# A hybrid encoder on one core: the S5 mixer in chunks of four tokens instead of eight, two groups to a matmul

## The chip, the cores and the metric

The kernel runs on one core of one Trainium2 chip. The metric is the device time of one execution in microseconds (us). The core has five engines that run their own instruction queues in order: TensorE (PE in the profile; PEld is its loading of weights), VectorE (DVE), ScalarE (ACT), GpSimd (POOL) and SyncE (SP, which here only issues DMAs).

## The reference

A trunk of two layers works on 272 tokens (16 meta tokens and 256 inputs) of 2048 features in float32. Each layer has a token mixer, half of it attention and half of it a bidirectional S5 scan, and then a channel mixer, which is dense in layer 0 and two-of-eight experts in layer 1. The S5 half is what the change touches:

```python
def s5_direction(u_c, lam_re, lam_im, log_step, b_re, b_im, c_re, c_im, reverse):
    lam = lax.complex(lam_re, lam_im)                       # per group (64) and state (64)
    dt = jnp.exp(log_step)[:, None]
    lam_bar = jnp.exp(lam * dt)
    b_bar = ((lam_bar - 1.0) / lam)[..., None] * b          # states x 16 channels
    bu = jnp.einsum('gpc,blgc->blgp', b_bar, u_c)
    a = jnp.broadcast_to(lam_bar, bu.shape)
    _, h = lax.associative_scan(combine, (a, bu), axis=1, reverse=reverse)
    return jnp.real(jnp.einsum('gcp,blgp->blgc', c, h))     # 16 channels of each group
```

It runs forwards and backwards, the two are added with `d_skip * u`, and a gelu and a gate follow before the output projection.

## The kernel before

The program is five stages: layer 0's mixers (`mixer`), layer 0's output projection and dense mixer (`mixer_end`, `dense`), layer 1's mixers, its output projection with the router, and the experts (`moe`). Large products run as three float32r products of split weights and split inputs; weights stream from DRAM through `Stream` and are split by ACT (`wh`) and DVE (`wl`). In layer 0's mixers the weights are used as float32 as they come (`raw`).

The order of all instructions is fixed when the program is built. `Sched` runs one main generator and side generators, keeps a model of when each engine would get to the work, and lets a side task emit its next piece once its operands should be there. `LEAD` holds how far DVE may run ahead of TensorE for each side task. On the chip each engine then takes its instructions in that order, so an instruction that is not ready holds up all that stands behind it on its engine.

S5 works in chunks of `TC` = 8 tokens, `NC` = 34 chunks, for 64 groups of 16 channels, with 64 complex states in each direction (128 rows: forward states on partitions 0 to 63, backward on 64 to 127):

- `prep` makes powers 0 to 8 of the discretized eigenvalues, on DVE.
- `v_load` and `v_make` make V, a chunk's 8 x 16 inputs to the states, two groups at a time: two DMAs of 256 KB (`pscr` and `ssm_bT`) and four DVE products of 128 x 512 and 128 x 256.
- `ssm_x` multiplies V (128 x 128, real and imaginary) by the group's inputs U (128 x 34): what each chunk adds to the states, X.
- `ssm_scan` steps through the chunks on DVE: four products of 128 x 128 for each of the 32 steps. Each step needs the one before it.
- `w_all` makes W (states to outputs), and from it with small matmuls (`toep`, 64 x 160) M, a chunk's inputs to its own outputs. Both go through DRAM (`wscr`, `escr`, `mscr`).
- `ssm_y` makes each group's outputs with three matmuls, chunks on partitions: states before the chunk H (128 x 34) by W (128 x 128), twice, and U by M. `turn` transposes them.

For layer 1 V, W and M are made during layer 0's dense mixer (`ahead`) and read back (`ssm_v1`, `ssm_w`). In both layers x stands between the input products, the scan mostly within attention, and y within the first half of the output projection (`w_out`, half 0), ahead of the gate.

Of the kernel before, what the change touches and what calls it, by code (L numbers as in the profile page):

```python
# [9 lines left out]
F32 = mybir.dt.float32  # L10
# [14 lines left out]
NC = 34  # L25
TC = 8
VG = 2
SLACK = 6000.0
NRAW = 40
VQ = 3  # L30
XHEAD = 0
# [5 lines left out]
        "prep1": 400.0, "v1": 800.0, "w1": 700.0, "scan1": 100.0, "gate": 2125.0}  # L37
# [4 lines left out]
# the router's constants  # L42
MLOW, MTOK, MTRI, MIO = 0, 64, 72, 200
NMC = 328
# expert 0's first rows of features
# [19 lines left out]
class Arena:  # L65
    """Columns of one float32 tile, handed out and taken back in emission order."""
# [23 lines left out]
    def room(self, *ws):  # L90
        """Whether pieces of these widths can all be had."""
# [46 lines left out]
class Stream:  # L138
    """The weights in the order of use: loaded ahead, and split into two float32r parts unless they are
    taken as they are."""  # L140
# [63 lines left out]
    def tend(self):  # L204
        """What can be done ahead without a long wait."""
# [34 lines left out]
class Model:  # L240
    """When each engine gets to the work emitted so far, by what the work's operands wait for."""
# [9 lines left out]
    def where(self, ap):  # L251
        """The region of ap, in units of a few columns of a partition quarter."""
# [13 lines left out]
        else:  # L266
# [3 lines left out]
            if sb:  # L270
                row = n // tn.shape[0]
                p0, f0 = divmod(off, row)
                np_ = pat[0][1] if len(pat) else 1
# [22 lines left out]
    def ready(self, *aps):  # L296
        """When what was emitted will have been written into aps."""
# [7 lines left out]
    def clear(self, ap):  # L305
        """When what was emitted will be done with ap."""
# [68 lines left out]
class Eng:  # L375
    """An engine whose work is timed as it is emitted."""
# [68 lines left out]
class Sched:  # L445
    """Emission order: main work, with side work where its operands should be there.

    A generator yields None, a time of the tensor engine to wait for, a condition, or the name of
    a backlog of the vector engine to wait for."""
# [19 lines left out]
    def add(self, gen, urgent=None):  # L469
        """A side task; with urgent, one that fills idle time until urgent()."""  # L470
# [56 lines left out]
class Kern:  # L527
    def __init__(self, ctx, tc, A, out, dbg=None):
# [8 lines left out]
        self.pscr = [dp.tile([8, NG, 256], F32, name=f"pscr{l}") for l in range(2)]  # L537
        self.uscr = [dp.tile([8, 128, L], F32, name=f"uscr{l}") for l in range(2)]
        self.escr = [dp.tile([NG, 16, 240], F32, name=f"escr{l}") for l in range(2)]
        self.vscr = dp.tile([16, 128, 1024], F32, name="vscr")  # L540
        self.wscr = [dp.tile([16, 128, 1024], F32, name=f"wscr{l}") for l in range(2)]
        self.mscr = [dp.tile([128, NG, 128], F32, name=f"mscr{l}") for l in range(2)]
# [8 lines left out]
        self.Wp = self.pp.tile([128, 2, 10, NG], F32, name="Wp")  # L551
# [19 lines left out]
    def banks(self, **n):  # L571
        """Splits the banks of PSUM into rings."""
# [7 lines left out]
    def grab(self):  # L580
        """A bank of the shared ring that nobody holds."""
# [112 lines left out]
    def later(self, f, *aps):  # L694
        """Work whose operands are still being made."""
# [15 lines left out]
    def norm(self, ps, n, dst, flag):  # L711
        """dst = 1 / sqrt(ps + eps) once the sums in ps are there."""
# [1604 lines left out]
```

## Time and profile before

| what | before |
|---|---|
| median of 3 runs | 2624.03 us (2618.33 to 2628.5) |
| span of the profiled execution, first to last instruction | 2615.0 us |
| TensorE busy | 2540.2 us, 97% |
| DVE busy | 1950.8 us, 75% |
| ACT busy | 1349.5 us, 52% |
| mean granted TensorE clock | 0.986 |

No other time of the profiled execution is given; its span is 9.0 us under the median of the runs. All helpers record through one line (L403), so rows are told apart by operation, tile and shape. A float32 matmul has two records in the trace, a transpose one. "128*34 128x128" is a matmul with 128 rows, 34 columns of weights, and 128 columns that move. `fa` is the arena in which most tiles of S5 lie, `bank` a bank of PSUM.

### The profile page before, as it was taken

The page shows a single profiled execution, that of the slowest core. Times are in us where ns is not written, and L with a number is a line of the kernel's source. Part 1 is how long each engine was busy: PE and PEld are TensorE (multiplying, and loading weights), DVE is VectorE, ACT ScalarE, POOL GpSimd, SP SyncE. Part 2 cuts the span into 40 slices and gives each one's busy share as a digit, 9 for nine tenths or more (in the row PEclk, how much of TensorE's full clock was granted, in tenths as well). Part 3 has the DMA queues.
Part 4 walks back from the last instruction along what each step waited for, and adds up shares of the span by engine and source line. Part 5 has one row for each costly group of instructions (what it writes and reads, how often), then busy time and mean ns, then how long its engine had stood idle before and what let it go on. Part 6 is the DMA issues. An engine that isn't in the chain of part 4 may idle for free. (4 is left out here: it accounts for less than half of the span.)

```text
span 2615.0 us, 42822 instructions
## 1 busy us (share of the span) xinstructions
PE 2540.2 (97%) x16266; PEld 2276.0 (87%) x16266; DVE 1950.8 (75%) x3108; ACT 1349.5 (52%) x1850; POOL 12.7 (0%) x17
## 2 busy tenths in 40 slices
PE   8989999999999999999999999999999999999997
PEld 6766588999999999999999977898888888888886
DVE  7567883778777766666665476266999999999997
ACT  2112543543334333333344555355777777777775
POOL 0000000000000000000000000000000000000000
PEclk9998999999999999999999999999999999999998
DMA  6875275445888866566557724574999999999995
GB/s 210 201 213 182 75 244 195 159 161 179 276 272 276 268 196 213 192 200 213 191 171 216 213 105 149 174 292 165 381 342 385 358 341 386 354 336 374 356 342 194
DMA packets 266375, 637.36 MB, mean 244 GB/s; under 512 B 43489, under 2 KB 103265, under 8 KB 265009
## 3 DMA queue, kind: packets, MB, share of 16 engines
q1 hardware_dynamic: 263890, 622.42, 70.1%
q0 software_dynamic: 1552, 9.91, 1.1%
q8 instruction: 129, 2.11, 0.4%
q10 hardware_dynamic: 720, 2.23, 0.2%
q14 instruction: 84, 0.69, 0.1%
HBM read 599.85 MB, written 42.99 MB: 246 GB/s over the span
## 5 line engine op out<-in xcount | busy, mean ns | idle before, releaser
L403 DVE TENSOR_TENSOR wl<-raw,wh 128x1024 fp32r<-128x1024 f32 (+1 forms) x559 | 666.2, 1202 | 191.7 <-ACT wh L403 183.1
L403 ACT ACTIVATE wh<-raw 128x1024 fp32r<-128x1024 f32 (+1 forms) x559 | 579.4, 1040 | 307.0 <-PE bank L403 217.9
L403 PE MATMUL bank<-XH,wh 128*128 128x272 f32 (+1 forms) x2160 | 637.7, 295 | 0.5 <-ACT tmpr L403 0.5
L403 PE MATMUL bank<-XH,wl 128*128 128x272 f32 (+1 forms) x2160 | 623.4, 289 | 2.7 <-DVE wl L403 2.6
L403 PE MATMUL bank<-XL,wh 128*128 128x272 f32 (+1 forms) x2160 | 621.0, 287 | 1.6 <-DVE XL L403 1.3
L403 PEld LDWEIGHTS bank<-XH,wh 128*128 128x128 f32 x2160 | 407.4, 189 | 16.4 <-issue 14.5
L403 PEld LDWEIGHTS bank<-XH,wl 128*128 128x128 f32 x2160 | 407.2, 189 | 4.3 <-DVE wl L403 4.3
L403 PEld LDWEIGHTS bank<-XL,wh 128*128 128x128 f32 x2160 | 408.0, 189 | 2.5 <-DVE XL L403 2.2
L403 DVE TENSOR_TENSOR fa<-fa 128x256 f32<-128x256 f32 (+11 forms) x703 | 289.3, 425 | 108.9 <-DMA fa<-ssm_bT 60.2
L403 PE MATMUL bank<-fa 128*34 128x128 f32 (+10 forms) x2148 | 343.5, 302 | 25.3 <-DVE fa L403 17.9
L403 PEld LDWEIGHTS bank<-fa 128*34 128x34 f32 (+6 forms) x2148 | 267.9, 158 | 89.4 <-issue 33.6
L403 PE MATMUL bank<-ra,wh 128*128 128x272 f32 (+1 forms) x1792 | 342.9, 291 | 2.3 <-ACT wh L403 2.3
L403 ACT ACTIVATE fa<-bank 64x320 f32<-64x320 f32 (+8 forms) x281 | 138.4, 498 | 348.4 <-PE bank L403 315.2
L403 PEld LDWEIGHTS bank<-ra,wh 128*128 128x128 f32 x1792 | 281.8, 189 | 8.4 <-issue 4.6
L403 PE MATMUL bank<-ra,wl 128*128 128x272 f32 (+1 forms) x896 | 257.3, 287 | 0.8 <-DVE wl L403 0.8
L403 PE MATMUL bank<-wh,XH 128*128 128x512 f32 (+1 forms) x584 | 221.9, 380 | 0.7 <-ACT fa L403 0.4
L403 PE MATMUL bank<-wh,XL 128*128 128x512 f32 (+1 forms) x584 | 219.8, 376 | 0.0
L403 PE MATMUL bank<-wl,XH 128*128 128x512 f32 (+1 forms) x584 | 218.5, 374 | 0.0
L403 PE MATMUL bank<-wh,ra 128*128 128x512 f32 x552 | 185.0, 392 | 0.0
L403 PE MATMUL bank<-fa,raw 128*128 128x272 f32 x608 | 172.3, 425 | 8.5 <-DMA raw<-w_mix 7.4
L403 PEld LDWEIGHTS bank<-ra,wl 128*128 128x128 f32 x896 | 169.3, 189 | 1.0 <-DVE wl L403 1.0
L403 DVE TENSOR_TENSOR wl<-h,wh 128x1024 fp32r<-128x1024 f32 (+1 forms) x137 | 157.0, 1156 | 10.0 <-ACT wh L403 7.4
(118 smaller groups left out, 3053.2 us busy)
## 6 DMA issues: line engine op xcount, KB each, us to landing
raw<-w_dense SPq DMA_DIRECT2D x264, 512.0 KB
raw<-w_mix SPq DMA_DIRECT2D x150, 512.0 KB
raw<-w_moe_g SPq DMA_DIRECT2D x106, 512.0 KB
h<-w_moe_g SPq DMA_DIRECT2D x80, 512.0 KB
raw<-w_moe_d SPq DMA_DIRECT2D x73, 512.0 KB
h<-w_moe_d SPq DMA_DIRECT2D x59, 512.0 KB
raw<-w_moe_t SPq DMA_DIRECT2D x51, 384.0 KB
h<-w_moe_t SPq DMA_DIRECT2D x44, 384.0 KB
```

Of the source, the lines that this page charges most:

```text
L403: return f(*a, **k)
```

## The change

The chunk has four tokens (`TC` = 4, `NC` = 68). A group then has 4 x 16 = 64 input rows, and groups g and g + 32 share the 128 partitions: the rows of one at 0 to 63, of the other at 64 to 127. For x the inputs of both stand side by side with zeros in the other half (128 x 136), so one pair of matmuls serves two groups. The y matmuls stay three for each group, with 68 columns of weights (H, U) and 64 that move (W, M). The scan has 66 steps. `prep` needs powers 0 to 4. H is no longer one tile: `ssm_h` makes it for four groups at a time, with one copy of 64 x 536 on ACT and one on DVE, in a ring of two. U is loaded twice (`load_u`), for x and again for y, and the tiles of channels are taken in the order `TORD`. Two 128 x 1088 fills on POOL (`room_xu`) stand ahead of the first DMAs there. `LEAD` of the scan in layer 1 rises from 100 to 1200.

The program's instructions that change in number, both layers, before and after: x matmuls 256 and 128; y matmuls 384 and 384; `toep` matmuls 256 and 256; transposes of y 128 and 64; scan products on DVE 256 and 528; products of V 256 and 128; products of W 288 and 288 (of 320 or 640 columns, then 192 or 384); copies of X on ACT 64 and 128; copies into H 6 and 32 on either engine; DMAs on SP 2181 and 2037.

```diff
-NC = 34
-TC = 8
+NC = 68
+TC = 4
+NQ = NG // 2
+TORD = (0, 4, 1, 5, 2, 6, 3, 7)
+GW = (2, 4)
-        "prep1": 400.0, "v1": 800.0, "w1": 700.0, "scan1": 100.0, "gate": 2125.0}
+        "prep1": 400.0, "v1": 800.0, "w1": 700.0, "scan1": 1200.0, "gate": 2125.0}
...
+    def room_xu(self, F):
+        X = F.get([NC - 1, 2, NG], top=True)
+        U = Ring(Top(F), 2, [8, 2, NC])
+        for u in U.h:
+            self.nc.gpsimd.memset(u.ap, 0.0)
+        return X, U
+    def load_u(self, l, qb):
+        u = self.st["U"].next()
+        for hf in range(2):
+            self.nc.sync.dma_start(u[64 * hf:64 * hf + 64, :, hf],
+                                   rows(self.uscr[l], (4 * hf + qb) * 128 * L,
+                                        [[L, 16], [NC, TC], [16 * L, 8], [1, NC]]))
+        return u
...
-        for b in range(NG // VG):
+        for b in range(NQ // VG):
             pb, bt = got.pop(0)
             yield from self.v_make(l, v.ap, pb, bt)
...
+                    ps = bank[:, :4 * NC].rearrange("p (r h s) -> p r h s", r=2, h=2)
                     for r in range(2):
-                        nc.tensor.matmul(ps[:, g + i, r], v[:, i, r], U[:, b * 4 + g + i], start=True, stop=True)
+                        nc.tensor.matmul(ps[:, r].rearrange("p h s -> p (h s)"), v[:, i, r],
+                                         u[:, q + i].rearrange("p h s -> p (h s)"), start=True, stop=True)
...
+                    nc.scalar.activation(X[0:64, :, :, g::NQ].rearrange("p s r h -> p r h s"),
+                                         ps[0:64, :, :, 0:NC - 1], AF.Copy)
+                    nc.scalar.activation(X[64:128, ::-1, :, g::NQ].rearrange("p s r h -> p r h s"),
+                                         ps[64:128, :, :, 1:NC], AF.Copy)
...
+    def ssm_h(self, l, F):
...
+        for T in TORD:
+            for a in (0, 4):
+                yield lambda: n - st["hn"] < 2
+                t = rh.next()
...
+                nc.scalar.activation(t[0:64, :, :, 1:NC],
+                                     X[0:64, :, :, g:g + 4].rearrange("p s r g -> p g r s"), AF.Copy)
+                nc.vector.tensor_copy(t[64:128, :, :, 0:NC - 1],
+                                      X[64:128, ::-1, :, g:g + 4].rearrange("p s r g -> p g r s"))
...
-                    nc.tensor.matmul(ps[:, g], H[:, :, r, b * 4 + g], w[:, r, g], start=(r == 0), stop=False)
-                nc.tensor.matmul(ps[:, g], U[:, b * 4 + g], m[:, g], start=False, stop=True)
+                        nc.tensor.matmul(ps[:, a + g], H[:, g, r], w[:, b[0], r, :, b[1]], start=(r == 0), stop=False)
+                    nc.tensor.matmul(ps[:, a + g], u[:, a + g, T // 4],
+                                     m[:, a + g].rearrange("p (t c) -> p t c", t=TC), start=False, stop=True)
...
         for m in range(4):
             ps = self.psum("m")[:, :N]
             yield from self.gemm(ps, KD, *xq)
-            if m == 0 and raw:
+            if m == 0:
                 rue.free()
```

On TensorE in layer 1's input products, within x, there stood before (x matmuls are those of 34 columns, the rest are an input product):

```order
L403 MATMUL bank_70<-fa 128x34 x4
L403 MATMUL bank_67<-XH,wh_101 128x272
L403 MATMUL bank_67<-XL,wh_101 128x272
L403 MATMUL bank_67<-XH,wl_104 128x272
L403 MATMUL bank_69<-fa 128x34 x4
```

and now:

```order
L408 MATMUL bank_68<-fa 128x136 x2
L408 MATMUL bank_65<-XH,wh_102 128x272
L408 MATMUL bank_65<-XL,wh_102 128x272
L408 MATMUL bank_65<-XH,wl_105 128x272
L408 MATMUL bank_70<-fa 128x136 x2
```

A block of four matmuls becomes a block of two; either is for two groups. Before, two blocks shared a bank, now each has its own.

On TensorE at the first y of layer 1 there stood before (y matmuls are 34x128; DMAHW are the loads of W and M):

```order
L403 MATMUL bank_65<-XH,wl_106 128x256
L403 MATMUL bank_68<-fa 34x128 [waits DMAHW0_49]
L403 MATMUL bank_68<-fa 34x128
L403 MATMUL bank_68<-fa 34x128 [waits DMAHW1_49]
L403 MATMUL bank_68<-fa 34x128 x3
L403 MATMUL bank_65<-XH,wh_103 128x256
```

and now (y matmuls are 68x64):

```order
L408 MATMUL bank_66<-XH,wl_104 128x256
L408 MATMUL bank_71<-fa 68x64 [waits DMAHW4_49,DVE_49,Activation_49]
L408 MATMUL bank_71<-fa 68x64
L408 MATMUL bank_71<-fa 68x64 [waits DMAHW7_49,DMAHW5_49]
L408 MATMUL bank_71<-fa 68x64 x3
L408 MATMUL bank_66<-XH,wh_101 128x256
```

Before, 201 matmuls of the output projection stand between the last matmul of attention and this place, now 78 (39 in layer 0, before 189). The first y waits for DVE and ACT as well as for the loads.

On DVE after the last maximum of layer 1's attention (`TENSOR_REDUCE`) there stood before, up to H (the scan's steps are the rows with `L_93` and the row behind each):

```order
L403 TENSOR_TENSOR fa<-fa,sqr 128x256
L403 SCALAR_TENSOR_TENSOR XL<-bank_71,gn,XH 128x256
L403 TENSOR_TENSOR fa<-fa,sqr 128x256
L403 MEMSET fa 64x128 x2
L403 COPY fa<-fa 64x1408
```

and now:

```order
L408 TENSOR_TENSOR wl_106<-raw_97,wh_103 128x1024
L408 TENSOR_TENSOR fa<-L_93,fa 128x128 x2
L408 TENSOR_TENSOR fa<-fa 128x128 x2
L408 MEMSET fa 128x544 x2
L408 RECIPROCAL fa<-fa 128x256
L408 TENSOR_TENSOR tmpr<-bank_66,fa 128x256
L408 TENSOR_TENSOR h<-h,tmpr 128x256
L408 TENSOR_TENSOR wl_104<-raw_98,wh_101 128x1024
L408 COPY fa<-fa 64x8x67 x2
```

After that last maximum 7 steps of the scan follow before, 12 now; the last of them stands behind the first split of the output projection's weights. The reciprocal is that of attention's norm, for which the output projection's first result waits.

## Rows read from the trace of the kernel before

**Rows 1.** The page: TensorE and the other engines, busy time and share of the span, and in 40 slices of 65.4 us the granted clock of TensorE in tenths of full speed.

```profile
PE 2540.2 (97%) x16266; PEld 2276.0 (87%) x16266; DVE 1950.8 (75%) x3108; ACT 1349.5 (52%) x1850; POOL 12.7 (0%) x17
PEclk9998999999999999999999999999999999999998
```

**Rows 2.** Windows by stage: us from the span's start, length, then busy us (and instructions) of PE, PEld, DVE, ACT and POOL, granted clock, busy share of the DMA engines, GB/s. The stages are layer 0's input products with V, W and x (41 to 255), its attention (255 to 346), its output projection with y (346 to 447), the dense mixer and layer 1's input products (447 to 1480), layer 1's attention (1480 to 1600) and its output projection with y (1600 to 1700).

```profile
41.00:255.00 214.00, 186.59 (x858) 144.00 (x856) 140.98 (x331) 35.25 (x70) 0.00 (x0) 0.91 0.72 200
255.00:346.00 91.00, 87.62 (x396) 53.45 (x395) 76.70 (x290) 48.35 (x133) 0.00 (x0) 1.00 0.30 88
346.00:447.00 101.00, 101.00 (x793) 90.51 (x794) 52.62 (x109) 39.51 (x57) 0.00 (x0) 1.00 0.75 252
447.00:1480.00 1033.00, 1026.43 (x8045) 1010.57 (x8044) 716.80 (x1072) 432.78 (x565) 0.71 (x1) 1.00 0.67 213
1480.00:1600.00 120.00, 111.98 (x678) 90.94 (x677) 88.65 (x256) 70.24 (x156) 0.00 (x0) 0.97 0.31 108
1600.00:1700.00 100.00, 100.00 (x812) 89.59 (x811) 38.85 (x58) 37.26 (x51) 0.00 (x0) 1.00 0.54 183
```

**Rows 3.** Waits from 41 to 255 us: who waited for whom, us in total, times, longest.

```profile
DVE fa L403 <- DMA fa<-ssm_bT: 47.5, 21, 6.1
PEld bank L403 <- DVE fa L403: 25.2, 15, 3.6
PE bank L403 <- DVE fa L403: 16.6, 10, 3.2
```

**Rows 4.** Groups of TensorE by shape (records, busy us, mean ns of one): x, y, `toep`, the transposes of y.

```profile
L403 PE MATMUL bank<-fa 128*128 128x34 f32 x512 | 68.4, 278 | 14.3 <-DVE fa L403 13.1 <-issue 1.2
L403 PE MATMUL bank<-fa 128*34 128x128 f32 x768 | 96.6, 277 | 0.0
L403 PE MATMUL bank<-fa 128*64 128x160 f32 x512 | 85.2, 310 | 5.2 <-DVE fa L403 3.5 <-DVE XL L403 1.7
L403 PE MATMUL bank<-cst,fa 34*128 34x34 f32 x128 | 10.9, 227 | 0.0
```

**Rows 5.** TensorE in order of time: start, us, shape, records merged. The pitch of a block is the time to the next row's start by the number of records.

```profile
31.79 7.04 PE L403 MATMUL bank<-fa,raw 128*128 128x272 f32 x30
38.76 0.71 PE L403 MATMUL bank<-cst,fa 64*128 64x64 f32 x8
...
941.91 1.30 PE L403 MATMUL bank<-fa 128*64 128x160 f32 x8
943.14 0.51 PE L403 MATMUL bank<-ra,wh 128*128 128x272 f32 x2
...
1434.37 0.97 PE L403 MATMUL bank<-fa 128*128 128x34 f32 x8
1435.18 0.37 PE L403 MATMUL bank<-XH,wh 128*128 128x272 f32 x1
...
1630.49 1.53 PE L403 MATMUL bank<-fa 128*34 128x128 f32 x12
1631.95 0.68 PE L403 MATMUL bank<-cst,fa 34*128 34x34 f32 x8
1632.57 1.53 PE L403 MATMUL bank<-fa 128*34 128x128 f32 x12
```

**Rows 6.** Groups of DVE and ACT by shape: V (the first, and most of the second), the scan (the next two), the copies into H on DVE; then the copies of X on ACT, which write with a stride, a plain copy of as many columns, and the copies into H on ACT.

```profile
L403 DVE TENSOR_TENSOR fa<-fa 128x512 f32<-128x512 f32 x128 | 88.2, 689 | 63.5 <-DMA fa<-ssm_bT 60.2 <-DMA escr<-fa 1.0 <-DVE fa L403 0.4
L403 DVE TENSOR_TENSOR fa<-fa 128x256 f32<-128x256 f32 x136 | 51.6, 420 | 1.9
L403 DVE TENSOR_TENSOR fa<-fa 128x128 f32<-128x128 f32 x128 | 36.8, 287 | 2.2
L403 DVE TENSOR_TENSOR fa<-L,fa 128x128 f32<-128x128 f32 x128 | 31.0, 283 | 2.5 <-ACT fa L403 2.1
L403 DVE COPY fa<-fa 64x1408 f32<-64x1408 f32 x6 | 9.7, 1617 | 0.2
...
L403 ACT ACTIVATE fa<-bank 64x272 f32<-64x272 f32 x64 | 41.0, 640 | 57.8 <-PE bank L403 57.2
L403 ACT ACTIVATE fa<-bank 128x272 f32<-128x272 f32 x44 | 19.4, 444 | 24.6 <-PE bank L403 23.3 <-DVE fa L403 1.1
L403 ACT ACTIVATE fa<-fa 64x1408 f32<-64x1408 f32 x6 | 8.2, 1367 | 0.0
```

**Rows 7.** DVE in order of time at the end of layer 1's attention: the scan's last step, the first copy into H, the reciprocal of attention's norm, the first result of the output projection.

```profile
1594.29 0.61 DVE L403 TENSOR_TENSOR fa<-fa 128x128 f32<-128x128 f32 x2
...
1596.46 1.62 DVE L403 COPY fa<-fa 64x1408 f32<-64x1408 f32 x1
...
1601.35 1.75 DVE L403 RECIPROCAL fa<-fa 128x256 f32<-128x256 f32 x1
1603.21 0.42 DVE L403 TENSOR_TENSOR tmpr<-bank,fa 128x256 f32<-128x256 f32 x1
```

**Rows 8.** POOL at the start, in order of time.

```profile
1.28 0.74 POOL L385 DMA_DIRECT2D gn<-gn  x1 [0.83 <-POOLq L2309]
2.57 1.21 POOL L769 MEMSET Wp<- 128x1280 f32 x1
```

**Rows 9.** DMA issues: what, how many, KB each; the two loads for V.

```profile
fa<-pscr SPq DMA_DIRECT2D x64, 256.0 KB
fa<-ssm_bT SPq DMA_DIRECT2D x64, 256.0 KB
```

More of the change, by code (lines that the diff above doesn't have):

```diff
@@ L272, in where @@
                 p0, f0 = divmod(off, row)
-                np_ = pat[0][1] if len(pat) else 1
+                np_ = (pat[0][1] - 1) * max(pat[0][0] // row, 1) + 1 if len(pat) else 1
                 quarters = range(p0 // 32, (p0 + np_ - 1) // 32 + 1)
@@ L907, in prep @@
         idn = self.cst[:64, CI:CI + 64]
-        src = [(Pb[:, m, r], m, r) for r in range(2) for m in range(9)] + [(Pw[:, 8, r], 9, r) for r in range(2)]
-        for b in range(0, 20, 8):
+        n1 = TC + 1
+        src = [(Pb[:, m, r], m, r) for r in range(2) for m in range(n1)] + [(Pw[:, TC, r], n1, r) for r in range(2)]
+        for b in range(0, len(src), 8):
             bank = yield from self.grab()
@@ L1000, in ssm_v1 @@
         rv = Ring(F, 3, [4, 2, 128])
-        for b in range(NG // 4):
+        for b in range(NQ // 4):
             yield lambda: n * b - st["vn"] < 3 * n - n + 1
@@ L1012, in ssm_x, with inputs @@
         nc, st = self.nc, self.st
-        X, U = st["X"], st["U"]
-        for b in range(NG // 4):
-            bank = None
-            if b % 8 == 0:
-                yield self.has("U", l, b // 8)
-                yield self.rdy(U[:, b * 4:b * 4 + 32])
-            for g in range(0, 4, VG):
+        X = st["X"]
+        st["xu"] = {}
+        def inputs():
+            for qb in range(4):
+                yield lambda: qb - st["xb"] < 2
+                yield self.has("u", l, qb)
+                yield self.has("u", l, qb + 4)
+                yield max(self.rdy(self.uscr[l][qb]), self.rdy(self.uscr[l][qb + 4]))
+                u = self.load_u(l, qb)
+                st["xu"][qb] = u, self.rdy(u)
+        st["xb"] = 0
+        self.s.add(inputs())
+        for qb in range(4):
+            yield lambda: qb in st["xu"]
+            u, t = st["xu"][qb]
+            yield t
+            for q in range(0, 8, VG):
                 yield lambda: len(st["vq"]) > 0
@@ L1070, in w_all @@
         NB = NG // G
+        S = TC + 2
         yield self.has("prep", l)
-        n = G * (640 + 320 + 160 + 16 + 256) + 512 + 64
+        ns = (2 * 2 * G * S * 16, 2 * 256, 2 * G * 128, 2 * G * S * 16, G * S * 16, NG, G * 16)
+        n = sum((x + 15) // 16 * 16 for x in ns)
         yield lambda: F.room(n)
@@ L1090, in w_all @@
         for b in range(2):
-            got[b] = load(b, 8, rc, "ssm_C")
-            gotz[b] = load(b, G, rz, "ssm_bz")
-        sh = [128, G, 10, 16]
+            got[b] = load(8 * TORD[b], 8, rc, "ssm_C")
+            gotz[b] = load(first(b), G, rz, "ssm_bz")
+        sh = [128, S, G, 16]
         def toep(b, w):
@@ L1210, in ssm_y @@
         N, k0 = L - q0, q0 // TC
-        yield self.has("H", l)
-        yield st["tH"]
-        H, U = st["H"], st["U"]
-        yield lambda: self.R is not None and F.room(8 * N, 1024, 1024) and self.R.room(8 * N, 8 * N)
+        yield self.has("scan", l)
+        yield lambda: "rh" in st and self.R is not None and F.room(8 * N, 512, 512) and self.R.room(8 * N, 8 * N)
         R = self.R
@@ L1279, in pace @@
             return self.s.now() + PACEV * VG / 4, lambda: len(kept) >= b
-        yield from self.v_all(l, F, put_v, pace, False)
-        yield from self.w_all(l, F, 4, PACEW)
+        yield from self.v_all(l, F, put_v, pace, lambda: len(kept))
+        yield from self.w_all(l, F, GW[1], PACEW)
     def rope(self, dst, src, c0, n, done):
@@ L1340, in mixer @@
             add(self.w0(F))
+        st["accs"] = None if raw else [F.get([L]) for _ in range(2)]
         cqf, ckf = F.get([4, N]), F.get([2, L])
-        st["accs"] = None if raw else [F.get([L]) for _ in range(2)]
         st["acc"] = acc = None if raw else st["accs"][0].ap
         r_in = F.get([L])
-        U = st["U"] = F.get([NG, NC], top=True)
-        st["X"] = F.get([NC, 2, NG], top=True)
+        st["X"], st["U"] = self.xu if raw else self.room_xu(F)
         rue = Ring(F, 2, [TC, NC])
@@ L1397, in u_tile @@
             self.post(lambda: put_u(T, ue), ue)
-        for T in range(8):
-            yield from u_tile(T)
+        for i, T in enumerate(TORD):
+            yield from u_tile(i, T)
         if raw:
@@ L1437, in mixer @@
         yield self.has("kv", l)
-        for t in (rq, rk, r_in) if raw else (rq, rk, cqf, ckf):
+        for t in (rq, rk, r_in) + (() if raw else (cqf, ckf)):
             t.free()
@@ L1512, in mixer @@
         ns = self.ns = self.psum("n")
-        acc = None if raw else self.Wp.rearrange("p r s g -> p (r s g)")[:, BLK:]
+        acc = None if raw else self.Wt[:, BLK:]
         for m in range(8):
@@ L1526, in w0 @@
         yield self.has("V0", 0)
-        yield from self.w_all(0, F, 2, 0)
+        yield from self.w_all(0, F, GW[0], 0)
     def mixer_end(self, l, F):
```

281 lines of the change are left out of this document (145 added, 136 removed).

## The prediction

> **What bounds the kernel now.** I read the page first. TensorE is busy for 97% of the span [rows 1], so a microsecond taken from its queue should come off the time, unless TensorE waits in that stage for something else. So the next view is the windows by stage [rows 2]. The reader is to see three kinds of stage there. In the dense mixer and layer 1's input products (447 to 1480 us) TensorE is busy for 1026 of 1033 us at full clock; in the two output projections with y (346 to 447, 1600 to 1700) for all of it. In layer 1's attention 8 of 120 us are idle. Layer 0's input products (41 to 255) are different: 187 of 214 us busy at a granted clock of 0.91, with the DMA engines busy for 0.72 at 200 GB/s. The waits of that stretch [rows 3] say why: DVE waits 47.5 us for the loads of V, and TensorE waits 16.6 and 25.2 us for DVE. Last I read what S5 costs TensorE, by shape [rows 4] and, since matmuls overlap, by pitch [rows 5]: x 0.81 / 8 = 0.101 us a record, `toep` 1.23 / 8 = 0.154, y 1.46 / 12 = 0.122, y's transposes 0.62 / 8 = 0.078, and the float32 product of 272 columns 6.97 / 30 = 0.232. Each layer has half the records of rows 4: x 256, y 384, `toep` 256, transposes 64. That is 26 + 47 + 39 + 5 = 117 us of TensorE in each layer.
>
> **The change on TensorE, for each layer.** New shapes are not in the trace, so each gets two ends.
> - x: 128 records of 136 columns. Half of the 272-column pitch is 0.116; the ends are 0.101 (as now, 128 columns of weights to load) and 0.130 (y's 0.122 for 128 columns, by 136 / 128). I take 0.116: 25.9 - 14.8 = 11 us less (9 to 13).
> - `toep`: 256 records of 96 columns instead of 160. By columns 0.154 x 0.6 = 0.092; the ends are 0.154 (nothing gained) and the transposes' 0.078. I take 0.092: 16 us less (0 to 19).
> - y: 384 records, with 68 columns of weights instead of 34 and 64 that move instead of 128. The ends are 0.061 (half of now) and 0.101 (x, whose moving part is so small that its weights must set the pitch). The nearest row is the small transposes at 0.078, which holds the change-over to the next block too; I take 0.07: 20 us less (8 to 23).
> - Transposes: 32 for 64, of twice the columns: 2 us less.
>
> A rule speaks against y here. The row shows 0.122 us with 34 columns of weights [rows 5], and these double. The Trainium skill, "TensorE: Matmul & The Clock Gate", section "LDWEIGHTS (loading the stationary operand)", says that loading time goes with the columns of the stationary operand, about columns / 1.2 ns. Worked out from that, an estimate for 68 columns is 57 ns, twice that of 34, and still under my 70; by it alone y would give 25 us a layer rather than 20 and the sum would be 10 us lower. The pitch of x, 0.101 for 128 columns, agrees with it within 6%.
>
> **Stage by stage.**
> 1. Layer 0 up to 346 us. TensorE's own part is x and `toep`, 27 us. The other view is bytes: V takes 16 batches for 32, and a batch is 2 x 256 KB [rows 9], so 8.4 MB less, which is 42 us at 200 GB/s [rows 2]. Against that, the order asks for V and W in a shorter stretch, so the queue can be as late as now while it lasts; the low end is 15 us. With the 42 us that TensorE waited for DVE halving in number I take 36 us. At the start POOL fills two tiles of 1088 columns ahead of the load of the gains; 1.21 us for 1280 [rows 8] makes 2 x 1.03, so 2 us later, since the first product waits for the gains. Sum: -34 (-13 to -40, and -59 if the clock also came back to its upper level, 214 x 0.09 = 19).
> 2. Layer 0's projection with y: -22, and +3 for H (below): -19 (-7 to -25).
> 3. Dense mixer: layer 1's `toep` stands there, and nothing else is waited for: -16 (0 to -19). V and W of layer 1 become shorter on DVE, which costs and gives nothing: DVE is busy 717 of 1033.
> 4. Layer 1's x: -11. ACT's copies of X double in number, 32 to 64 a layer, at the strided price of 0.64 us for about as many columns as now [rows 6]: +20 us of ACT, which also splits the weights. Eight groups' worth of copies (10 us) come against some 7 us of TensorE; four PSUM banks and the split ahead take most of it. +3 (0 to +10): -8.
> 5. Layer 1's attention, with the scan. A step is (36.8 + 31.0) / 64 = 1.06 us [rows 6], the two rows being all steps of both layers. 34 more a layer are 36 us of DVE, serial. In exchange V loses half of (88.2 + 48.6) / 2 = 68 us a layer. In layer 0 the scan starts while the input products still run, and ends before attention does. In layer 1 25 steps stand between the first and the last maximum of attention instead of 11, which is 15 us more on a DVE that is busy for 89 of 120 us, and 12 behind the last one instead of 7: 5 us more ahead of the reciprocal of attention's norm, which ended at 1603.1 and for which the first result of the projection waits [rows 7]. PSUM gives TensorE three results' room. +3 (0 to +13).
> 6. Layer 1's projection with y: as 2, -19.
>
> H in 2 and 6: 16 copies on each of ACT and DVE a layer, 536 columns. From 1.617 and 1.367 us for 1408 [rows 6] that is 0.62 and 0.52; a strided ACT copy costs 0.64 for 0.444 plain [rows 6], so up to 0.9 and 0.75. A pair of copies must fit into the time of four groups on TensorE (24 records x 0.07 and six of the projection, 2.5 us), with the evacuations of y and the gelu beside them on ACT. It fits, with little to spare, so 3 us of waits each. What is queued behind a y that waits for H is the rest of the projection; the order puts 39 and 78 matmuls of it ahead of the first y, 5 and 10 us at the 0.128 us a record of the dense stage [rows 2].
>
> Sum: -34 - 19 - 16 - 8 + 3 - 19 = -93 us. Against the span of 2615.0 that is 2522; the median of the runs lies 9.0 above the span, so 2531 us. For this kernel about 0.5% (13 us) can be told from no change.
>
> **The rivals.**
> - Half of it. The loads of V stay late because they come more densely (20 us instead of 36), the small matmuls have a floor near 0.09 us (y 12 a layer with its waits, `toep` 10), ACT eats half of x's gain, and attention loses 5: -18 - 24 - 10 - 5 + 5 = -52, 2572 us. For it: DVE already waits for V's loads at 200 GB/s [rows 3], and no float32 matmul in rows 5 is under 0.1. Against: the transposes at 0.078, and windows 2 and 6 with DMA far from full.
> - More of it. Layer 0's input products were set by the loads alone, and with them gone TensorE stays at the upper clock: stage 1 gives 59 - 2 us, the rest as above: 2508 us. Against: the raw weights go through the same queue.
> - It does not do what it says: the sums of columns shrink, but each record costs what it did (x apart), and the copies into H and the scan take the rest. About -10, 2614 us. Against: x alone has half the records.
> - Slower: the scan on DVE. Twice the steps stand in the same queue as attention's maxima, and every maximum of its 40 tiles waits for one step (1.06 us each, 42 us); the steps that find no gap end behind attention, 36 us less the 5 and 10 us of cover, so 26 to 31 a layer, and TensorE stands at the first y, since nothing behind it can pass; H then sets the pace of y, 16 a layer instead of the gain of 20. That is 42 + 57 in waits and 40 of lost gain, against 93: +46, 2670 us. It decides from about 50 us of such waits for a loss of y's gain. For it: before, the scan's last step ended 1.6 us ahead of the first copy into H, with the scan throttled to attention's pace [rows 7]. Against: in layer 0's attention DVE did 77 of 91 us of work with the scan in it, and TensorE was busy for 88 of 91 [rows 2].
>
> **How the numbers follow.** The forecast, 2500 to 2560, 0.57; more, 0.10; half, 0.22; no change 0.05; slower 0.06. So faster by over 0.5% 0.89, within 0.5% 0.05, slower 0.06. The forecast's own range is 2500 to 2560; to hold 8 in 10 it takes in half of it and part of more: 2495 to 2592.
>
> **What will show it.** Layer 0's projection should begin near 313 instead of 347 us, and TensorE's waits for DVE before it should be about half. In the rows by shape, `68x64` should take about 27 us a layer of TensorE (384 x 0.07), `128x136` about 15, `64x96` about 24. The dense mixer, from first to last matmul, should be 16 us shorter. In the two projections TensorE should stay busy for all but a few us; if it waits there for ACT or DVE `fa` at the y matmuls, H is dearer than I took it. If the pitch of y is 0.1 or more, or if TensorE's idle time in the attentions grows by more than 10 us, the forecast is wrong in that term.

## The result and the profile after

The changed kernel takes 2530.9 us (median of 4 runs, 2522.9 to 2534.6) against 2624.9 for the kernel before (4 runs): a ratio of 0.964, 95% interval 0.961 to 0.967. The forecast was 2531. That the two agree is partly luck, as the stages show: the two output projections gained 23 us more than forecast, and layer 1's input products with attention lost 24 us where 5 less were forecast.

The profiled executions are 82 us apart (spans 2615.0 and 2532.8), the medians 94: single executions of a kernel differ by up to 12 us, and the one of before was a short one. Each run of the changed kernel lies 1.8 us above its own span, so most of the 9.0 that the forecast added to the span of before stood for this spread.

The stages are cut at the same matmuls in both traces: the first of layer 0's output projection, of the dense mixer, of layer 1's input products, of layer 1's output projection, and of the router. The windows of the kernel before (columns as in [rows 2], but other cuts):

```profile
7.00:346.70 339.70, 307.37 (x1393) 224.04 (x1394) 249.95 (x704) 99.84 (x243) 0.74 (x1) 0.94 0.59 171
346.70:459.50 112.80, 112.80 (x890) 102.41 (x889) 60.68 (x119) 43.56 (x61) 0.00 (x0) 1.00 0.71 238
459.50:1391.00 931.50, 924.93 (x7209) 909.13 (x7208) 669.76 (x1020) 387.21 (x509) 0.71 (x1) 1.00 0.66 212
1391.00:1594.40 203.40, 195.38 (x1381) 174.34 (x1379) 121.60 (x285) 106.37 (x199) 0.00 (x0) 0.99 0.52 160
1594.40:1699.10 104.70, 104.70 (x836) 94.24 (x836) 43.55 (x66) 41.18 (x56) 0.00 (x0) 0.98 0.55 189
1699.10:2615.00 915.90, 895.04 (x4566) 771.88 (x4564) 801.79 (x896) 668.41 (x779) 8.56 (x8) 0.99 0.89 329
```

The same windows of the changed kernel:

```profile
9.00:310.40 301.40, 280.40 (x1313) 202.18 (x1314) 233.38 (x817) 118.95 (x285) 1.14 (x2) 0.96 0.52 157
310.40:389.50 79.10, 76.46 (x802) 75.65 (x801) 51.35 (x74) 48.94 (x59) 0.00 (x0) 1.00 0.59 175
389.50:1305.10 915.60, 910.99 (x7202) 899.38 (x7201) 610.88 (x943) 381.72 (x494) 1.10 (x2) 1.00 0.59 193
1305.10:1532.10 227.00, 196.20 (x1252) 168.78 (x1250) 148.81 (x414) 126.53 (x230) 1.95 (x2) 0.94 0.37 122
1532.10:1609.50 77.40, 76.03 (x803) 75.20 (x803) 53.52 (x86) 49.87 (x61) 0.00 (x0) 0.97 0.59 185
1609.50:2532.80 923.30, 896.90 (x4566) 774.45 (x4565) 802.59 (x896) 668.92 (x779) 8.47 (x8) 0.98 0.88 326
```

| stage | before | after | change | forecast |
|---|---|---|---|---|
| up to layer 0's projection | 346.7 | 310.4 | -36 | -34 |
| layer 0's projection with y | 112.8 | 79.1 | -34 | -19 |
| dense mixer | 931.5 | 915.6 | -16 | -16 |
| layer 1's input products and attention | 203.4 | 227.0 | +24 | -5 |
| layer 1's projection with y | 104.7 | 77.4 | -27 | -19 |
| gate, router, experts | 915.9 | 923.3 | +7 | 0 |

The fourth window is the one to read. TensorE is busy for 196 us as before, though x has half the matmuls: its granted clock fell from 0.99 to 0.94, and 5% of 196 us is 10, about what x saves. And its idle time grew from 8 to 31 us. The groups of TensorE by shape in that window (first x in the kernel before, then of the changed kernel x and two kinds of waits for DVE):

```profile
L403 PE MATMUL bank<-fa 128*128 128x34 f32 x256 | 31.2, 267 | 0.0
...
L408 PE MATMUL bank<-fa 128*128 128x136 f32 x128 | 21.5, 293 | 13.3 <-DMA fa<-uscr 6.5 <-issue 3.8 <-ACT fa L408 2.9
L408 PE MATMUL bank<-XH,wl 128*128 128x256 f32 x64 | 19.1, 298 | 2.0 <-DVE wl L408 2.0
L408 PE MATMUL bank<-fa 128*128 128x272 f32 x32 | 11.5, 443 | 3.6 <-DVE XL L408 3.6
```

Before, x waited for nothing. Now it stands 13.3 us, of which 10.3 are the first matmul of three of the four quarters: two of these waits (6.5) are put down to the load of U, the third (3.8) to "issue", with SP's orders for U ahead of it as in the others. One of them, by engine in order of time (SP's issues, then TensorE, both of the changed kernel):

```profile
1336.68 0.33 SPq L390 DMA_DIRECT2D uscr<-fa  x1
1341.32 0.33 SPq L390 DMA_DIRECT2D raw<-w_mix  x1
1341.76 1.26 SPq L390 DMA_DIRECT2D fa<-uscr  x2
...
1347.39 0.70 PE L408 MATMUL bank<-fa 128*128 128x136 f32 x4 [3.48 <-DMA fa<-uscr]
```

An input product for U goes out to DRAM at 1336.7 and is ordered back at 1341.8; x needs it, and stands in TensorE's queue 3.5 us too early. Windows of 10 us from x on, in the columns of the stage windows:

```profile
1390.00:1400.00 10.00, 10.00 (x74) 10.00 (x73) 1.65 (x2) 9.76 (x16) 0.00 (x0) 0.83 0.17 58
...
1410.00:1420.00 10.00, 7.96 (x62) 7.69 (x60) 9.72 (x28) 2.36 (x4) 0.00 (x0) 0.97 0.36 120
1420.00:1430.00 10.00, 8.32 (x65) 7.98 (x63) 9.83 (x25) 4.87 (x8) 0.00 (x0) 1.00 0.32 105
...
1510.00:1520.00 10.00, 8.11 (x26) 4.04 (x25) 7.36 (x32) 4.35 (x13) 0.00 (x0) 0.82 0.01 2
1520.00:1530.00 10.00, 9.63 (x27) 5.52 (x26) 9.50 (x40) 4.29 (x12) 0.00 (x0) 0.50 0.00 1
```

They show three things: ACT full (9.76 of 10) in a block of x, where TensorE is busy throughout at a clock of 0.83; then DVE full (9.7, 9.8) with the scan's steps between the splits of the weights, and TensorE idle for some 2 us in each; and at the end of attention, after TensorE was busy for 8.1 us of 1510 to 1520, a granted clock of 0.50, the lower of its two levels.

S5 on TensorE by shape, both layers, and then in order of time (changed kernel):

```profile
L408 PE MATMUL bank<-fa 128*68 128x64 f32 x768 | 57.1, 225 | 4.0 <-ACT fa L408 3.4 <-issue 0.4 <-DVE fa L408 0.2
L408 PE MATMUL bank<-fa 128*64 128x96 f32 x512 | 56.6, 254 | 8.7 <-DMA fa<-ssm_bz 8.5 <-ACT fa L408 0.2
L408 PE MATMUL bank<-fa 128*128 128x136 f32 x256 | 42.7, 293 | 19.1 <-DMA fa<-uscr 11.9 <-issue 4.3 <-ACT fa L408 2.9
```

```profile
43.38 0.87 PE L408 MATMUL bank<-fa 128*64 128x96 f32 x8
44.18 0.72 PE L408 MATMUL bank<-fa,raw 128*128 128x272 f32 x2
...
52.22 0.63 PE L408 MATMUL bank<-fa 128*128 128x136 f32 x4
52.68 0.62 PE L408 MATMUL bank<-fa,raw 128*128 128x272 f32 x2
...
315.58 0.90 PE L408 MATMUL bank<-fa 128*68 128x64 f32 x12
316.28 0.37 PE L408 MATMUL bank<-XH,wh 128*128 128x272 f32 x1
```

The pitches, to be held against [rows 5], are 0.80 / 8 = 0.100 us for `toep` (0.154), 0.46 / 4 = 0.115 for x (0.101 for twice as many), and 0.70 / 12 = 0.058 for y (0.122). In the rows by shape a block's busy time holds its last record to the end (0.22 to 0.29 us), so there x has 21 us a layer, `toep` 28 and y 29, where the prediction named 15, 24 and 27.

### The profile page after: what moved, and what is told of

The parts are those of the page before. It is cut to its first block, busy times and chain, and to the rows that moved or that the text cites. A ratio compares the mean times of both kernels' runs of the same rounds, so it can differ in the third digit from the quotient of the medians.

```text
span 2532.8 us, 42146 instructions
## 1 busy us (share of the span) xinstructions
PE 2437.0 (96%) x15930; PEld 2195.6 (87%) x15930; DVE 1906.0 (75%) x3250; ACT 1396.5 (55%) x1908; POOL 17.2 (1%) x23
## 5 line engine op out<-in xcount | busy, mean ns | idle before, releaser
L408 PE MATMUL bank<-fa 128*68 128x64 f32 (+11 forms) x1892 | 258.4, 276 | 38.1 <-DMA fa<-uscr 11.9
L408 PEld LDWEIGHTS bank<-fa 128*68 128x68 f32 (+5 forms) x1892 | 193.0, 159 | 97.9 <-issue 55.6
L408 DVE TENSOR_TENSOR fa<-fa 128x128 f32<-128x128 f32 (+9 forms) x687 | 236.6, 353 | 41.0 <-ACT fa L408 22.3
L408 ACT ACTIVATE fa<-bank 64x268 f32<-64x268 f32 (+8 forms) x313 | 159.4, 514 | 176.8 <-PE bank L408 158.6
L408 PE MATMUL bank<-fa,raw 128*128 128x272 f32 x608 | 167.0, 414 | 9.5 <-ACT fa L408 9.5
```

Of the source, the lines that this page charges most:

```text
L408: return f(*a, **k)
```

## The experiments

All start from the changed kernel, and where the text says so from an earlier run; `...` in a diff stands for lines left out. Stage times are from one profiled execution each and cut as above. Layer 0's first stage, in kernels that have the very same instructions there, took 304 to 314 us, so only larger differences are read in it. Layer 1's input products with attention took 225 to 231 us in the four kernels that have the changed kernel's instructions there in the same order (itself, the one with more loads for V, and the two on the pitch of y), so a difference under some 6 us can be spread there too. The others repeat within 3 us where nothing of them is edited; the last one lies within 919 to 924.

Four runs hold back the copies into H by a stricter condition on free room, which is not printed: the two with fewer steps of the scan, the one with three instructions a step, and the lead of 2500. No run has this condition alone.

**Where layer 1's 24 us come from.**

```diff
             u, t = st["xu"][qb]
-            yield t
+            yield t + 4500.0
```

> Layer 1's input products with attention came out 23.6 us longer where 5 shorter were forecast. x of a quarter (eight pairs of groups) stands in TensorE's queue 4.5 us (by the planner's count) later than in the changed kernel, in both layers; nothing else is edited. Theory 'round trip': x stands too close behind the input product that it needs, since that goes out to DRAM and comes back (write 4.1 us, load 3.7 us), and TensorE stood for it 10.3 us in layer 1 and 5.4 in layer 0: these waits go, 8 to 14 us less. Theory 'scan': what counts in layer 1 is when the scan ends; x 4.5 us later makes the scan and attention as much later, so the gain in layer 1 is given back: 0 to 4 us less.

2519.0 us, ratio 0.959 (0.957 to 0.962). Layer 1's stage fell from 227.0 to 215.2; x no longer waits for U, and of the 2.2 us of waits that are left 2.1 are for ACT:

```profile
L408 PE MATMUL bank<-fa 128*128 128x136 f32 x128 | 20.5, 284 | 2.2 <-ACT fa L408 2.1
```

Layer 0's stage took 306.8, within its spread. The round trip holds, for layer 1: 12 us (10 to 16 by the spread of that stage).

```diff
-        "prep1": 400.0, "v1": 800.0, "w1": 700.0, "scan1": 1200.0, "gate": 2125.0}
+        "prep1": 400.0, "v1": 800.0, "w1": 700.0, "scan1": 100.0, "gate": 2125.0}
```

> The lead of layer 1's scan goes back from 1200 to 100 ns, the value of the kernel before: fewer steps of the scan stand ahead of the splits of the weights. Theory 'scan': between x and attention DVE is busy for 97% and TensorE stands 10 us behind splits that wait behind steps of the scan; with the lead of 100 these waits fall to under 4 us, but the steps come later, 10 or more of them behind attention's last maximum: between 6 us less and 15 us more. Theory 'round trip': the lost time is at x, the order of the scan matters little: within 4 us of the changed kernel.

2549.2 us, ratio 0.971 (0.968 to 0.973). Layer 1's stage fell to 210.2 us, 17 less, but the projection rose from 77.4 to 109.4. The y matmuls there:

```profile
L408 PE MATMUL bank<-fa 128*68 128x64 f32 x384 | 28.9, 239 | 31.9 <-DVE fa L408 25.0 <-ACT fa L408 6.9
```

TensorE stood 25 us for DVE, the end of the scan and H. That is the mechanism of the forecast's slower rival; the higher lead, part of the change, is what avoids it.

```diff
-        for s in range(1, NC - 1):
+        for s in range(1, (NC - 1) // 2 + 1 if l == 1 else NC - 1):
...
```

> Leaves out the second half of the scan's steps in layer 1 (33 of 66), so that its output is not the reference's; the copies into H begin as late as before by a stricter condition on free room. 33 steps are 35 us of DVE. Theory 'scan': DVE sets layer 1's input products behind x and attention (8.8 of 10 us busy in each stretch of 10), so 12 to 25 us go there, the dip of TensorE's clock at the end of attention with it. Theory 'round trip': DVE's work there is mostly beside TensorE, 0 to 6 us less.

2522.1 us, ratio 0.960 (0.957 to 0.962). Layer 1's stage fell by 8 us to 218.6 (7 to 13 by its spread), less than the scan theory asked or at its low end, and a little more than the other did: 35 us of DVE are worth about a quarter of that to TensorE.

For the next run `prep` lays out `L8` by input and output, with as many instructions as before, so that one product makes four.

```diff
-            TT(t1.ap, self.L8[:, 0], X[:, s - 1], op=OP.mult)
-            TT(t2.ap, self.L8[:, 1], X[:, s - 1, ::-1], op=OP.mult)
-            TT(X[:, s], X[:, s], t1.ap, op=OP.add)
-            TT(X[:, s], X[:, s], t2.ap, op=OP.add)
+            TT(t1.ap, self.L8, X[:, s - 1].rearrange("p i (o g) -> p i o g", o=1).to_broadcast([128, 2, 2, NG]), op=OP.mult)
+            TT(X[:, s], X[:, s], t1[:, 0], op=OP.add)
+            TT(X[:, s], X[:, s], t1[:, 1], op=OP.add)
...
```

> A step of the scan takes three instructions of DVE for four: one product of 128 x 256 (0.42 us) for two of 128 x 128 (2 x 0.29), so 0.15 us less a step, 10 us of DVE in each layer; the result is the same. Theory 'scan': 3 to 8 us less in layer 1, nothing in layer 0. Theory 'round trip': within 2 us.

2535.5 us, ratio 0.966 (0.963 to 0.969), no gain. The wide product did take 0.420 us for 2 x 0.285, yet layer 1's stage took 231.0, the upper end of its spread. A cheaper step changes the planner's order too, and the copies into H are held back; this run can't part these. So it is inconclusive, and the 3 to 8 us that the scan theory asked are not seen.

**Which of the two leads.** On top of x later, a lead of 500:

```diff
-        "prep1": 400.0, "v1": 800.0, "w1": 700.0, "scan1": 1200.0, "gate": 2125.0}
+        "prep1": 400.0, "v1": 800.0, "w1": 700.0, "scan1": 500.0, "gate": 2125.0}
```

> x 4.5 us later, as in the run before, and the lead of layer 1's scan 500 ns for 1200. The lead of 100 alone took 17 us off layer 1's input products and attention and put 32 us onto the projection, where TensorE stood 25 us at the first y. Theory 'a scan of 70 us has to fit between x and y, and the lead only chooses who waits': 0 to 10 us slower than x later alone (2519). Theory 'there is room between': the waits at the input products fall by 5 to 10 us and the scan still ends before the first y: 2509 to 2515 us.

2531.3 us, ratio 0.963 (0.961 to 0.966): layer 1's stage 207.7 (7.5 less than x later), the projection 99.3 (22 more). The lead chooses who waits, and there is no room between; the price was larger than expected.

**ACT at x.** Also on top of x later:

```diff
-                    nc.scalar.activation(X[64:128, ::-1, :, g::NQ].rearrange("p s r h -> p r h s"),
-                                         ps[64:128, :, :, 1:NC], AF.Copy)
+                    xb = X[64:128, ::-1, :, g::NQ].rearrange("p s r h -> p r h s")
+                    if l in (1,):
+                        nc.vector.tensor_copy(xb, ps[64:128, :, :, 1:NC])
+                    else:
+                        nc.scalar.activation(xb, ps[64:128, :, :, 1:NC], AF.Copy)
```

> x 4.5 us later, and in layer 1 the backward half of the copies of X goes from ACT to DVE, which is busy for under 4.5 of 10 us there, while ACT is busy for 9.8 of 10 us in the blocks of x. Theory 'ACT paces x': the waits of x for ACT (2.1 us with x later) go, and the splits of the weights come earlier: 2 to 5 us less than x later alone. Theory 'ACT only catches up afterwards': within 2 us.

2511.5 us, ratio 0.956 (0.953 to 0.959), the fastest with the reference's result, and faster than both kernels. Layer 1's stage took 211.3, 4 less than with x later alone, which its spread could give too. The intervals of the two ratios overlap, but all four runs (2509.3 to 2515.3) lie under all four of x later (2517.2 to 2520.5). So a gain is likely, and its size in the stage, about 4 us, is not secured.

The next two start from this run. First 32 steps of the scan in layer 1, so that the output is not the reference's:

```diff
-        for s in range(1, NC - 1):
+        for s in range(1, 33 if l == 1 else NC - 1):
...
```

> x 4.5 us later and the backward copies of X on DVE in layer 1, and there the scan stops after 32 steps of 66 (so that the output is not the reference's), the number of the kernel before. Layer 1's input products and attention took 203.3 us before, 227.0 in the changed kernel, 211.3 with the two edits. Theory 'three causes' (x too close to its product, copies of X on ACT, 34 more steps of the scan): the stage comes to 200 to 205 us, 6 to 11 less than with the two edits. Theory 'the clock, or something not named': it stays above 208.

2507.6 us, ratio 0.955 (0.953 to 0.957). Layer 1's stage came to 202.8 us, where the kernel before had 203.4: with the load of U, ACT's copies and the 34 added steps taken out, the loss is gone. But x's own 11 us of gain is still not to be seen in it. Here is the window, and TensorE's waits for DVE's sums and splits in it:

```profile
1309.50:1512.30 202.80, 187.84 (x1252) 165.25 (x1250) 140.86 (x319) 103.23 (x198) 1.95 (x2) 0.96 0.42 136
...
PE bank L408 <- DVE fa L408: 7.5, 4, 2.4
PE bank L408 <- DVE wl L408: 5.1, 4, 1.9
```

TensorE is busy 7.5 us less than before, and idle for 15 us where it was for 8; the two waits were 3.8 and 1.0 us before. On DVE, early steps of the scan, let in by the lead of 1200, stand ahead of those splits and sums.

Second, the lead at 2500, with all steps:

```diff
-        "prep1": 400.0, "v1": 800.0, "w1": 700.0, "scan1": 1200.0, "gate": 2125.0}
+        "prep1": 400.0, "v1": 800.0, "w1": 700.0, "scan1": 2500.0, "gate": 2125.0}
...
```

> x 4.5 us later, the backward copies of X on DVE in layer 1, and the lead of layer 1's scan 2500 ns for 1200, with the stricter condition on room for H. Leads of 500 and 100 moved waits from the input products to the first y and cost 12 to 18 us. Theory 'the lead only chooses who waits, and at 1200 y waits for nothing': the steps come earlier still, the splits of the weights later, 2 to 10 us more than 2511. Rival, 'the scan's end still delays the reciprocal of attention and with it the projection': 2 to 6 us less.

2527.1 us, ratio 0.963 (0.961 to 0.965): layer 1's stage 226.0 instead of 211.3, the projection 77.9 as it was. That is 15.6 us more in the median, where 2 to 10 were expected. More lead than 1200 only adds waits here; less moves them to y.

**What layer 0's first stage was made of.**

```diff
+        for _ in range(2 if l == 0 else 0):
+            x = self.st["spare"].next()
+            self.nc.sync.dma_start(x.rearrange("p g r m -> p (g r m)"),
+                                   rows(self.A["ssm_bT"], l * 32 * NQ * 256 + b * n,
+                                        [[NQ * 256, 32], [0, TC], [1, n]]))
...
```

> With each of layer 0's 16 batches of V two more loads of 256 KB into a place that nothing reads, 8.4 MB in all: the bytes of the kernel before, with the halved work of DVE and TensorE. Theory 'bytes' (half of the forecast's first term): the loads set layer 0's input products, so 15 to 42 us come back there (42 by bytes at 200 GB/s) and DVE waits for the loads again. Theory 'engines': the first term came from TensorE's own x and toep and from DVE's halved products, the queue has room (its share was 0.52): under 6 us come back.

2566.4 us, ratio 0.977 (0.974 to 0.980). The dense mixer began at 422.6 us instead of 389.6. DVE's wait for V is back (first 310 us: this kernel, then the changed kernel with TensorE's wait for DVE):

```profile
DVE fa L408 <- DMA fa<-ssm_bT: 46.1, 12, 11.3
...
DVE fa L408 <- DMA fa<-ssm_bT: 4.5, 5, 1.7
PEld bank L408 <- DVE fa L408: 4.6, 10, 0.9
```

It was 47.5 us before [rows 3]. So with the old bytes the two stages take 33 us more. Not all of that need be the bytes' own, since the planner's order moved too: the projection began at 296 us, 14 earlier, and then took 126.5 instead of 79.1. It holds 120 records of `toep` (about 12 us) that stood ahead of it, waits of y for W and of `toep` for DVE, and its granted clock is 0.85.

This run starts from the one with x later and half of the copies on DVE (2511.5 us):

```diff
-                if b + 1 < NB:
-                    gotz[b + 1] = load(first(b + 1), G, rz, "ssm_bz")
+                if b + 2 < NB:
+                    gotz[b + 2] = load(first(b + 2), G, rz, "ssm_bz")
...
```

> x 4.5 us later, the backward copies of X on DVE in layer 1, and the ring of loads for toep (ssm_bz) three deep, each load ordered a batch earlier. In the changed kernel TensorE stood 8.5 us for these loads in layer 0's input products. Theory 'TensorE paces layer 0': 4 to 8 us less than with the two edits (2511). Theory 'layer 0 waits elsewhere by then' (DVE, the queue of loads): within 3 us.

2540.4 us, ratio 0.968 (0.965 to 0.970): 29 us slower than without the deeper ring, outside both expectations. TensorE's waits for these loads went, but the planner set the last products of W between steps of the scan on DVE, and `toep` waited for them:

```profile
210.04 0.58 PE L408 MATMUL bank<-fa 128*64 128x96 f32 x2 [2.22 <-DVE fa L408]
210.97 1.22 PE L408 MATMUL bank<-fa 128*64 128x96 f32 x6 [0.35 <-DVE fa L408]
```

In the window around it TensorE is busy for 7.3 of 20 us, DVE for 19, and the granted clock falls to 0.61:

```profile
200.00:220.00 20.00, 7.34 (x36) 4.96 (x37) 19.05 (x79) 1.29 (x4) 0.00 (x0) 0.61 0.22 62
```

**What sets the pitch of y.** Two kernels, one execution each.

```diff
-                    for r in range(2):
-                        nc.tensor.matmul(ps[:, a + g], H[:, g, r], w[:, b[0], r, :, b[1]], start=(r == 0), stop=False)
+                    for lo, hi in ((0, 64), (64, NC)):
+                        for r in range(2):
+                            nc.tensor.matmul(ps[lo:hi, a + g], H[:, g, r, lo:hi], w[:, b[0], r, :, b[1]],
+                                             start=(r == 0), stop=False)
...
```

> Each y matmul of 68 columns of weights is made as one of 64 and one of 4 (outputs on partitions 0 to 63 and 64 to 67), with the same 64 columns that move; 768 y matmuls a layer for 384, in records 768 for each shape. The pitch of y in the changed kernel is 0.70 / 12 = 0.058 us a record. Theory 'weights': the pitch goes with the columns of weights, 0.058 x 64 / 68 = 0.055 and 0.003; a block of 24 records stays near 0.70 us. Theory 'floor': a small float32 matmul takes 0.05 to 0.06 us whatever its weights; a block of 24 records takes 1.3 us or more, and each projection is 20 us longer.

```profile
314.88 1.91 PE L408 MATMUL bank<-fa 128*64 128x64 f32 x24
316.72 0.39 PE L408 MATMUL bank<-XH,wh 128*128 128x272 f32 x1
```

1.84 / 24 = 0.077 us a record; the projections took 115.6 and 113.9 us, 36.5 more each. The row merges two shapes: six records with 64 columns of weights, six with 4, and both again. Taken apart (the end of a six of 64, the six of 4, the start of the next; then the mean ns of one of each):

```profile
315.10 0.34 PE L408 MATMUL bank<-fa 128*64 128x64 f32 x3
...
315.37 0.50 PE L408 MATMUL bank<-fa 128*4 128x64 f32 x6
...
315.80 0.39 PE L408 MATMUL bank<-fa 128*64 128x64 f32 x3
...
L408 PE MATMUL bank<-fa 128*64 128x64 f32 x768 | 72.1, 230 | 0.3 <-DMA fa<-mscr 0.2
L408 PE MATMUL bank<-fa 128*4 128x64 f32 x768 | 63.8, 219 | 0.0
```

A row lasts until the end of its last record, so the pitch in the six of 4 is (0.50 - 0.22) / 5 = 0.056 us, and between the last three of 64 (0.34 - 0.22) / 2 = 0.06. From the last record of 64 (two pitches behind 315.10, at 315.22) to the first of 4 it is 0.15 us, and as much from there back. So the 0.077 is no pitch: each block of 24 holds four changes of shape at 0.15 us, the last of them to the next matmul.

```diff
+                    for j in (0, 2):
+                        for r in range(2):
+                            nc.tensor.matmul(ps[:, a + g, j:j + 2], H[:, g, r], w[:, b[0], r, j:j + 2, b[1]],
+                                             start=(r == 0), stop=False)
...
```

> Each y matmul of the changed kernel is made as two, each with all 68 columns of weights and 32 of the 64 columns that move. With the weights split (64 and 4 columns) a block of 24 records took 1.75 us, not 0.70, so the weights alone do not set the 0.058 us a record. Theory 'columns that move': 0.232 us for 272 columns makes 0.027 for 32, a block of 24 records takes 0.70 us and the projections stay near 79 us. Theory 'floor': a record costs 0.055 or more with 32 columns too, a block of 24 takes 1.3 us or more and each projection is 20 us or more longer.

```profile
318.27 1.61 PE L408 MATMUL bank<-fa 128*68 128x32 f32 x24
319.71 0.37 PE L408 MATMUL bank<-XH,wh 128*128 128x272 f32 x1
```

1.44 / 24 = 0.060, and the projections took 99.6 and 98.8, about 21 more each. With half the columns that move a record costs the same, as the floor theory said; but each still has 68 columns of weights, so this run can't tell a floor from the weights. The rows together fit the larger of two times, one by the columns of weights and one by the columns that move. Within a block, 68 columns of weights take (0.90 - 0.22) / 11 = 0.06 with 64 that move and (1.61 - 0.22) / 23 = 0.06 with 32; 128 with 34 that move took 0.101 [rows 5]; and 4 with 64 that move take 0.056, where 64 columns at the pitch of the 272-column product (0.232 / 272 = 0.85 ns a column) are 0.054. A floor just under 0.06 is neither shown nor excluded by this: no run has few columns of both.

## Why the prediction came out as it did

- **x, `toep`, y on TensorE: right.** x was taken at 0.116 and took 0.115. `toep` was taken at 0.092 and took 0.100, so 14 us a layer for 16; the dense mixer gave the 16 us forecast. y was taken at 0.07 and took 0.058: 384 x 0.064 = 24.5 us a layer for 20. Of the 15 us that layer 0's projection gave beyond the forecast, 9 are `toep`: 56 records at 0.154 stood in that stage before and stand ahead of it now, where the forecast had booked all of them.
- **The reason for y's pitch: it agrees with the rows, and a floor close by is not excluded.** The prediction put x's pitch down to its columns of weights, and y's 68 fit roughly the same line: 0.101 for 128, 0.06 for 68. By the Trainium skill ("TensorE: Matmul & The Clock Gate", "LDWEIGHTS (loading the stationary operand)"), whose time goes with the columns of weights, the estimate was 0.057 us for 68, and 0.058 was measured. The forecast's 0.07, from the small transposes, was the poorer choice. The expectation of the run with 64 and 4 columns of weights gave the weights' theory 0.70 us for a block, which took 1.84; it left out that 64 columns still move in each record (0.056 with 4 columns of weights) and the 0.15 us for each change of shape. The Trainium skill, on the same page under "Back-to-back issue gap", has for up to 64 columns that move a floor of about 25 ns, and of about 62 ns a matmul if instructions aren't decoded in hardware; the 0.056 lies between the two, so the second does not bind a record here. The rival of half the gain named a floor near 0.09; records came down to 0.056.
- **Layer 0's first stage: right in size, and by the term that was in doubt.** The first product began at 9.5 us for 7.4, the 2 us forecast for POOL's fills. DVE's wait for the loads of V fell from 47.5 to 4.5 us, and TensorE's waits for DVE, 42 us before, to about 7; the forecast had half. With the old bytes put back 33 us return, over this stage and the projection, in an order that moved as well, so how much of the 36 is the loads' own is not shown. The fallen wait speaks against the rival in which these loads stay late because they come more densely; and the clock rose only from 0.94 to 0.96, not to the upper level throughout, as the rival of more gain had it.
- **H: right.** TensorE waited 2.6 and 1.4 us at y, forecast 3 each. The copies were dearer on ACT than the bound (1.15 us, taken at up to 0.9; 0.78 on DVE), and still fitted.
- **Layer 1's input products and attention: wrong, by 28 us.** The step that failed is the sum of stages 4 and 5, which priced what was counted and left out what was moved. The load of U for x had no term: x for a quarter now needs the input products of two tiles out to DRAM and back, and 12 us of waits were its price, where x waited for nothing before. TensorE's idle time in the stage grew by 23 us, 13 of them at x; 10 in the attentions was the prediction's own sign of being wrong in that term. The lead of the scan, raised from 100 to 1200, had none either. ACT's copies were taken at +3 and cost about 4, within the spread of the stage; the 34 steps at +3 (0 to 13) and cost some 8. From 203.4 these make 203.4 - 11 + 12 + 4 + 8 = 216; the rest up to 227 is put down to the early steps of the lead by the run with a lead of 100 (17 us less; 8 of these are taken to be the added steps, which that lead moves out of the stage). This is a sum over separate runs, each with a spread of up to 6 us, and was not tried in one kernel.
- **The rival on the slower side** did not come about, and its place was right: with the old lead TensorE stood at the first y for the scan's end, 25 us, as the rival said.
- **The experts: 7 us more, open.** All other profiles of the new scheme have 919 to 924 us there, the one of before 915.9, with the same 4566 records of TensorE. One short execution of before can't tell a cost from spread, and no run was made for it.

So the total was met by errors that cancel: 23 us too little in the two projections, 28 too much in layer 1's stage, and a profiled execution of before that was short.

## What to carry to other kernels

When a change regroups work, list what each new block needs and when the last piece of it exists: a block for two tiles waits for the second, and a trip through DRAM is then no longer covered by the work between. Of a number that only steers the order, such as a lead, ask which queue it moves work past, and put a price on it like on any instruction. Of a small matmul ask which is larger, its columns of weights or the columns that move: shrinking the other gains nothing, and splitting either into more matmuls costs, with a change of shape on top. And read a mean over a block that mixes shapes only after taking it apart.

## What the runs showed that was not expected

A float32 matmul of S5 takes 0.06 us a record with 68 columns of weights, whether 64 or 32 columns move, and 0.056 with 4 and 64. A change between matmuls of 64 and of 4 columns of weights takes 0.15 us; these also write to other partitions of the bank, and which of the two makes it dear stays open. Freeing DVE gives little by itself: 35 us of it were worth some 8 us of the stage, and of three instructions for four in each step no gain was seen. A ring made one deeper cost 29 us, by the order that the planner then chose.
